# Moving VectorE's additions on product banks, and the sample rows' sums, behind the next unit's parts in a hybrid decoder step

## The chip, the cores and the metric

The kernel runs on one core of one Trainium2 chip. The metric is the device time of one execution in microseconds (us). One execution was taken by the hardware profiler as well; its rows give the start and length of every instruction on TensorE (PE; its weight loads are PEld), VectorE (DVE), ScalarE (ACT), GpSimd (POOL) and the DMA queue of SyncE (SP).

## The reference

One layer of a decoder trunk is computed for 2048 prompt tokens and for 64 sample tokens (8 sequences of 8). A gated recurrence and a short convolution share one input projection; their outputs go through an output projection and a LayerNorm, and then the MLP follows, in which most of the arithmetic lies:

```python
D_MODEL = 1024; SEQ = 2048; DEC_BATCH = 8; DEC_SEQ = 8; D_FF = 4 * D_MODEL

def _layer(x, s_hgrn, conv_buf, ...):
    proj = jnp.einsum('btd,dp->btp', x, w_in)
    ...                                       # recurrence, short convolution, gates
    mix = jnp.einsum('btm,md->btd', jnp.concatenate([o, yc], axis=-1), w_out)
    x = _layer_norm(ALPHA * x + mix, ln1_g, ln1_b)
    hid = jnp.square(jax.nn.relu(jnp.einsum('btd,df->btf', x, w_ff1)))
    x = _layer_norm(ALPHA * x + jnp.einsum('btf,fd->btd', hid, w_ff2), ln2_g, ln2_b)
    return x, s_new, new_buf
```

All is float32. A float32 operand is split into a high part and the rest, and a product is made of three matmuls (high by high, high by low, low by high).

## The kernel before, in words

**Blocks.** The prompt goes in four blocks of 512 tokens (b = 0 to 3); the 64 sample tokens ride along in block 1. Per block come the input projection with the recurrence (phase m), the output projection with the first LayerNorm, and the MLP (phase f). The kernel is scheduled by hand: instructions stand on each engine in the order in which the Python code issues them, and every engine works through its own list in that order.

**The MLP.** The 4096 hidden columns are eight chunks c of 512. The first two chunks of a block (the first four in block 0) are made plainly by `ff1`. The others, and the whole second matrix, are made by seven block products of a 2 by 2 block scheme, named in `PRODUCTS` in the order T4, B11, B21, T2, T1, T3, B22. The chunks go in two parts of four. In a part, first come the first-matrix products of its chunks, seven *units* per chunk (`ff1_product`), and then the second-matrix products, a unit for every product and chunk (28 units, in the loop over `ff2_units`; 21 in the last part of block 3): first T4 for the four chunks, then B11 for the four, and so on. There are thus seven places where a run of `ff1_product` units ends and a run of second-matrix units begins: block 0 part 1, and both parts of blocks 1, 2 and 3.

**A unit's weights.** A unit uses one weight tile of 128 by 1024. `weights(u)` calls `ahead`, which keeps the splitting of weights four tiles ahead: it first runs all that waits in the list `later` (`flush`), and then ScalarE copies the tile that SyncE's DMA brought (`st`, three buffers) to the high part `wh` (L203), and the subtraction that makes the low part `wl` on VectorE (L210) is put into `later`. So the low part stands on VectorE's list only when the next unit begins. `st` is free for the next DMA when `wl` is made. `wh` and `wl` have four buffers each.

**What a first-matrix product leaves behind.** Its matmuls end in one of the PSUM banks D, A, C, B (eight banks in all, handed out in turn). `out(slot, op)` in `ff1_product` brings the bank into a quarter of the chunk's tile `raw`: for T4, B11, T2 and T1 as a copy by ScalarE (L1145); for B21 (one quarter), T3 (two quarters) and B22 (one quarter) as an addition by VectorE (L1147), issued at once behind the unit's matmuls. `sout` does the same for the 64 sample columns in block 1 (L1157). Behind such an addition the square of the rectified quarter (L1111, L1112, two ScalarE instructions) is put into `later`, after B22 also `chunk_done`, a subtraction between quarters on VectorE (L1044).

**What a second-matrix unit needs.** `prepare` splits a quarter of `raw`, two units before its use, into the high part `h` (ScalarE, L164) and the low part `l` (VectorE, L165, by way of `later`). The third matmul of a unit (L247) is the first that needs `l`. In block 1 the units of B11, B21, T1 and B22 also multiply the sample rows: their two parts stand side by side in the tile `hp`, made one unit ahead (L164, L165), and used at the unit's end (L250, L251). `X` is the next block's input, split in the same way between the weights.

**What a second-matrix product leaves behind.** After the last chunk of a product, additions to the output tiles (`add_to`, L1242 and L1245) go into the list `slow`, of which every following unit moves one entry (two if more than four are left) to `later`. `sample_sums` takes the sample rows' bank: ScalarE copies its upper 64 rows to `tmp` (L256), VectorE adds the lower 64 rows (L1252), both at once behind the matmuls, and the additions to the output rows (L1258, L1261) go into `slow`. There are eight such sums. `sum_rows` (L1234) makes sums of quarters that later products need.

**GpSimd in block 0.** It makes the tables of weight sums in DRAM (T_a, T_b) by DMA. To hold these transfers back, `hold` lets GpSimd read an element of slot 0 of `raw` (`tick`, L354) after each of the first eight `ff1_product` units of block 0, and issues one transfer behind it.

Of the kernel before, what the change touches and what calls it, by code (L numbers as in the profile page):

```python
# [14 lines left out]
ALU = mybir.AluOpType  # L15
# [9 lines left out]
NS = 64  # L25
# [4 lines left out]
ALPHA = float(2.0 ** 0.25)  # L30
# [31 lines left out]
def hybrid_step(ctx, tc, a, o):  # L62
    nc = tc.nc
    v, s, g, te = nc.vector, nc.scalar, nc.gpsimd, nc.tensor
# [26 lines left out]
    def TMP():  # L91

        return S((P, 4, P)) if phase["in"] == "m" else new((P, 4, P), "tmp", 2, F32, phase["of"])
# [14 lines left out]
    def PS(shape=(P, 512)):  # L108
        count[0] += 1
        return psum.tile(list(shape), F32, tag="ps", bufs=8, name=f"ps{count[0]}")  # L110
# [42 lines left out]
    later = []  # L153
# [89 lines left out]
    def mm3_on(out, lh, ll, rh, rl, first, last):  # L243

        te.matmul(out, lh, rh, start=first, stop=False, skip_group_check=True)  # L245
        te.matmul(out, lh, rl, start=False, stop=False, skip_group_check=True)  # L246
        te.matmul(out, ll, rh, start=False, stop=last, skip_group_check=True)  # L247
# [5 lines left out]
    def upper(bank):  # L253

        tmp = TMP().rearrange("p a b -> p (a b)")
        s.activation(tmp[:NS], bank[NS:2 * NS, :], AF.Copy)  # L256
        return tmp[:NS]
# [146 lines left out]
    for b in range(NB):  # L404
# [529 lines left out]
        def before():  # L934
            if lnq:
                for f in lnq[0][0]:
                    f()

        def after():
            if lnq:  # L940
                fs = lnq.pop(0)[1]
                if fs:
                    flush()
                for f in fs:
                    f()
# [83 lines left out]
        def sample_values(c, f):  # L1029
            part = c // NPART  # L1030
            if part not in rs:
                rs[part] = TOK().rearrange("p (f t) -> p f t", t=NS)
            return rs[part][:, f % (NPART * FC):f % (NPART * FC) + 2, :]

        def values(c):
            if c not in raw:

                raw[c] = F((P, 4, 2, 256), "raw", NPART)
            return raw[c]

        def chunk_done(c):

            r = raw[c]
            later.append(lambda: v.tensor_tensor(r[:, 0], r[:, 1], r[:, 0], ALU.subtract))  # L1044
# [65 lines left out]
        def relu2(z):  # L1110
            s.activation(z, z, AF.Relu)  # L1111
            s.activation(z, z, AF.Square)  # L1112
# [3 lines left out]
        def ff1_product(step, c, w):  # L1116

            wh, wl = w
            before()
            r = values(c)  # L1120
            k = to[step]
            if k not in fb:
                if samp and k != "D":
                    fb[k] = [PS()[:, :256 + NS] for _ in range(2)]
                else:
                    ps = PS((P, 2, 256))
                    fb[k] = [ps[:, q, :] for q in range(2)] + [ps]
                first = True
            else:
                first = False  # L1130
            banks_ = fb[k]
            xh_, xl_ = xq[step]
            n = 256 + NS if samp and step in SAMPLE else 256
            for kk in range(4):
                for q in range(2):
                    cs = slice(q * 512 + kk * P, q * 512 + kk * P + P)
                    mm3_on(banks_[q][:, :n], wh[:, cs], wl[:, cs], xh_[:, kk, :n], xl_[:, kk, :n],
                           first and kk == 0 and (q == 0 or len(banks_) == 2), kk == 3)

            def out(slot, op):  # L1140

                pairs_ = [(r[:, slot], banks_[2])] if len(banks_) == 3 else [(r[:, slot, q], banks_[q][:, :256]) for q in range(2)]
                for z, ps in pairs_:
                    if op < 2:
                        s.activation(z, ps, AF.Copy, scale=(1.0, -1.0)[op])  # L1145
                    else:
                        v.tensor_tensor(z, z, ps, (ALU.add, ALU.subtract)[op - 2])  # L1147

            def sout(half, op):
                if samp:  # L1150
                    z = sample_values(c, c * FC + 2 * half)
                    for q in range(2):
                        ps = banks_[q][:, 256:]
                        if op < 2:
                            s.activation(z[:, q, :], ps, AF.Copy, scale=(1.0, -1.0)[op])
                        else:
                            v.tensor_tensor(z[:, q, :], z[:, q, :], ps, ALU.add)  # L1157
                    if op == 2:
                        later.append(lambda: relu2(z))

            if step == "T4":
                out(0, 0)
            elif step == "B11":
                out(1, 0)
                sout(0, 0)
                sout(1, 1)
            elif step == "B21":
                out(1, 2)
                sout(0, 2)
                later.append(lambda: relu2(r[:, 1]))  # L1170
            elif step == "T2":
                out(3, 1)
            elif step == "T1":
                out(2, 1)
            elif step == "T3":
                out(2, 3)
                out(0, 2)
                later.append(lambda: relu2(r.rearrange("p (a b) q t -> p a b q t", b=2)[:, :, 0]))
            else:
                out(3, 3)  # L1180
                sout(1, 2)
                later.append(lambda: relu2(r[:, 3]))
                fb.clear()
                if b < NB - 1 or c < NCH - 1:
                    later.append(lambda: chunk_done(c))
            after()
# [60 lines left out]
        slow = []  # L1247

        def sample_sums(bank, into):

            up = upper(bank)
            v.tensor_tensor(up, up, bank[:NS, :], ALU.add)  # L1252

            def add(dh, sign):
                z = x1[NC][:NS, dh * 512:dh * 512 + 512]
                op = ALU.add if sign > 0 else ALU.subtract
                if (NC, dh) in touched:
                    v.tensor_tensor(z, z, up, op)  # L1258
                else:
                    touched.add((NC, dh))  # L1260
                    v.scalar_tensor_tensor(z, z, ALPHA, up, ALU.mult, op)  # L1261

            for dh, sign in into:
                slow.append(lambda dh=dh, sign=sign: add(dh, sign))

        for part, (ff1_units, ff2_units) in enumerate(pl["parts"]):
# [37 lines left out]
            for n_, (step, c, u) in enumerate(ff2_units):  # L1304
# [34 lines left out]
                if c == clast:  # L1339
                    for t0, dh, sign in INTO[k][step]:  # L1340
                        for p in range(2):
                            slow.append(lambda z=(t0 + p, dh, banks[k][p], sign): add_to(*z))
                    if samp and step in SAMPLE:
                        sample_sums(ys, SAMPLE[step][1])
# [7 lines left out]
        if b == NB - 1:  # L1352
# [21 lines left out]
            for t in range(nt):  # L1374
                for dh in range(2):
                    bank = PS()
# [110 lines left out]
```

## Time and profile before

| | |
|---|---|
| median of 3 runs | 2390.7 us (2389.76 to 2390.98) |
| the profiled execution | 2390.55 us, of which 2388.3 us is the span from the first to the last instruction |
| mean granted TensorE clock | 0.994 |
| busy: PE, PEld, DVE, ACT, POOL | 2340.0, 2043.1, 1785.6, 1233.5, 184.9 us |
| VectorE waiting for a product's last matmul, ahead of L1147 | 104.7 us in 57 waits |
| VectorE waiting for `tmp`, ahead of L1252 | 32.6 us in 8 waits |
| first-matrix units of block 2, part 1 | 1661.25 to 1741.88 us |
| second-matrix units of block 2, part 1 | 1741.88 to 1821.13 us |

In a row of the timeline stand an instruction's start in us from the start of the span, its length, engine, line, operation, the tile written and those read, and in brackets how long the engine had been idle before it and what ended that. The records of neighbouring matmuls overlap: in the second-matrix units one starts every 0.23 us and is shown with 0.39 us. So a stall of TensorE is read from the distance between starts; the idle time that a row shows is about 0.16 us less.

### The profile page before, as it was taken

To read this page: it belongs to the slowest core of one execution; us is meant where nothing else is said; L and a number is where in the kernel's file an instruction comes from. 1 tells how busy PE (TensorE), PEld (TensorE's weight loads), DVE (VectorE), ACT (ScalarE), POOL (GpSimd) and SP (SyncE) were. 2 spreads that over 40 slices of the span, in tenths; PEclk is the share of its full clock that TensorE was granted. 3 is DMA by queue.
4 is the path that set the end of the run, shared out by engine and by line. 5 is a ranking of instruction groups with operands and counts; after the bars stand their busy time and mean duration, and the time that the engine had idled before them with its cause. 6 is when DMAs were issued, how large, how long until landed. Compare 5 with 4: busy or idle time off the path is not lost.

```text
span 2388.3 us, 38146 instructions
## 1 busy us (share of the span) xinstructions
PE 2340.0 (98%) x15036; PEld 2043.1 (86%) x15036; DVE 1785.6 (75%) x2832; ACT 1233.5 (52%) x1922; POOL 184.9 (8%) x234
## 2 busy tenths in 40 slices
PE   8999999999999999999999999999999999999998
PEld 7778978988879889879878788998988788998996
DVE  7856858578785677875688956888588975888678
ACT  5324645565423446646654234665665324665563
POOL 2230021100101110000000000000000001000001
PEclk9999999999999999999999999999999999999999
DMA  8997598867633644545553325456665325456663
GB/s 285 264 282 214 151 266 273 257 200 211 163 107 78 172 149 133 168 150 177 177 177 109 99 71 194 155 187 197 192 210 163 102 79 172 141 176 203 200 191 119
DMA packets 131507, 418.89 MB, mean 175 GB/s; under 512 B 13376, under 2 KB 17856, under 8 KB 131328
## 3 DMA queue, kind: packets, MB, share of 16 engines
q1 hardware_dynamic: 108880, 347.96, 45.7%
q0 software_dynamic: 22016, 67.71, 11.5%
q8 instruction: 118, 1.93, 0.3%
q10 hardware_dynamic: 432, 0.79, 0.1%
q14 instruction: 61, 0.50, 0.1%
HBM read 405.36 MB, written 69.77 MB: 199 GB/s over the span
## 4 chain that ended last, share of the span: by engine, by line
PE 50%; DVE 5%; DMA 1%; issue 1%; ACT 1%; POOL 0%; POOLq 0%; DVEq 0%; ACTq 0%
PE ps L247 9%; PE ps L245 9%; PE ps L246 9%; PE ps L239 6%; PE ps L240 6%; PE ps L241 6%; DVE wl L210 1%; DMA st<-in_w_ff 1%; PE ps L683 1%; PE ps L250 1%; PE ps L251 1%; DVE S L603 0%; DMA st<-T_b 0%; DVE l L165 0%; ACT wh L203 0%
## 5 line engine op out<-in xcount | busy, mean ns | idle before, releaser
L210 DVE TENSOR_TENSOR wl<-st,wh 128x1024 fp32r<-128x1024 f32 x580 | 707.4, 1221 | 173.3 <-ACT wh L203 171.2
L203 ACT ACTIVATE wh<-st 128x1024 fp32r<-128x1024 f32 x581 | 612.9, 1055 | 352.1 <-PE ps L247 125.6
L239 PE MATMUL ps<-X,wh 128*128 128x256 f32 (+2 forms) x1376 | 466.6, 339 | 9.8 <-ACT X L164 8.3
L240 PE MATMUL ps<-X,wh 128*128 128x256 f32 (+2 forms) x1376 | 456.8, 332 | 0.3 <-DVE X L165 0.3
L241 PE MATMUL ps<-X,wl 128*128 128x256 f32 (+2 forms) x1376 | 456.3, 332 | 0.0
L247 PE MATMUL ps<-wh,l 128*128 128x512 f32 x868 | 340.8, 393 | 9.0 <-DVE l L165 8.6
L245 PE MATMUL ps<-wh,h 128*128 128x512 f32 x868 | 338.2, 390 | 0.0
L246 PE MATMUL ps<-wl,h 128*128 128x512 f32 x868 | 338.0, 389 | 0.0
L239 PEld LDWEIGHTS ps<-X,wh 128*128 128x128 f32 x1376 | 263.0, 191 | 35.0 <-ACT X L164 9.3
L241 PEld LDWEIGHTS ps<-X,wl 128*128 128x128 f32 x1376 | 262.8, 191 | 22.0
L240 PEld LDWEIGHTS ps<-X,wh 128*128 128x128 f32 x1376 | 263.2, 191 | 21.3 <-DVE X L165 1.5
L247 PEld LDWEIGHTS ps<-wh,l 128*128 128x128 f32 x868 | 162.9, 188 | 52.4 <-DVE l L165 19.0
L246 PEld LDWEIGHTS ps<-wl,h 128*128 128x128 f32 x868 | 163.0, 188 | 34.0
L245 PEld LDWEIGHTS ps<-wh,h 128*128 128x128 f32 x868 | 163.0, 188 | 33.1 <-ACT h L164 0.4
L165 DVE TENSOR_TENSOR l<-raw,h 128x512 fp32r<-128x512 f32 x217 | 148.2, 683 | 9.8 <-ACT h L164 9.8
L247 PE MATMUL ps<-X,wl 128*128 128x256 f32 (+1 forms) x528 | 152.1, 288 | 0.2 <-DVE wl L210 0.2
L246 PE MATMUL ps<-X,wh 128*128 128x256 f32 (+1 forms) x528 | 151.9, 288 | 0.0
L245 PE MATMUL ps<-X,wh 128*128 128x256 f32 (+1 forms) x528 | 151.9, 288 | 0.0
L271 POOL TENSOR_TENSOR sm<-sm,nhalf 128x1 f32<-128x1 f32 (+1 forms) x34 | 34.7, 1020 | 1475.8 <-DVE sm L270 1429.6
L1147 DVE TENSOR_TENSOR raw<-raw,ps 128x512 f32<-128x512 f32 (+1 forms) x112 | 61.0, 571 | 104.9 <-PE ps L247 104.7
L164 ACT ACTIVATE h<-raw 128x512 fp32r<-128x512 f32 x217 | 133.7, 616 | 2.3 <-PE ps L246 2.2
L239 PE MATMUL ps<-wh,X 128*128 128x512 f32 x256 | 105.8, 413 | 2.8 <-DVE S L603 2.8
(259 smaller groups left out, 4369.2 us busy)
## 6 DMA issues: line engine op xcount, KB each, us to landing
st<-in_w_ff SPq DMA_DIRECT2D x227, 512.0 KB, 3.7
st<-T_b SPq DMA_DIRECT2D x124, 512.0 KB, 3.7
st<-in_w_in SPq DMA_DIRECT2D x110, 512.0 KB, 3.9
st<-T_a SPq DMA_DIRECT2D x88, 512.0 KB, 3.5
st<-in_w_out SPq DMA_DIRECT2D x56, 512.0 KB, 4.5
T_b<-in_w_ff POOLq DMA_DIRECT2D x48, 512.0 KB, 14.7
T_a<-in_w_ff POOLq DMA_DIRECT2D x36, 512.0 KB, 19.1
T_b<-T_b POOLq DMA_DIRECT2D x16, 512.0 KB, 12.9
```

Of the source, the lines that this page charges most:

```text
L164: s.activation(hi, src, AF.Copy)
L165: later.append(lambda: v.tensor_tensor(lo, src, hi.bitcast(F32), ALU.subtract))
L203: s.activation(wh, st, AF.Copy)
L210: v.tensor_tensor(wl, st, wh.bitcast(F32), ALU.subtract)
L239: te.matmul(out, lh, rh, start=first, stop=False)
L240: te.matmul(out, lh, rl, start=False, stop=False)
L241: te.matmul(out, ll, rh, start=False, stop=last)
L245: te.matmul(out, lh, rh, start=first, stop=False, skip_group_check=True)
L246: te.matmul(out, lh, rl, start=False, stop=False, skip_group_check=True)
L247: te.matmul(out, ll, rh, start=False, stop=last, skip_group_check=True)
L271: g.tensor_tensor(st[:n, 15:16], st[:n, 14:15], nhalf[:n, 0:1], ALU.pow)
L1147: v.tensor_tensor(z, z, ps, (ALU.add, ALU.subtract)[op - 2])
```

## The change

Three things that stood at once behind a unit's matmuls are put into lists. The additions of `out` and of `sout` go into `later`, and so run when the next unit begins, behind the `wl` that is in the list already. In `sample_sums` ScalarE's copy of the upper rows goes into `later`, and VectorE's addition of the lower rows becomes an entry of `slow`, behind the `add_to` entries and ahead of the additions to the output rows.

```diff
@@ ff1_product: out, sout
                     if op < 2:
                         s.activation(z, ps, AF.Copy, scale=(1.0, -1.0)[op])
                     else:
-                        v.tensor_tensor(z, z, ps, (ALU.add, ALU.subtract)[op - 2])
+
+                        later.append(lambda z=z, ps=ps: v.tensor_tensor(z, z, ps, (ALU.add, ALU.subtract)[op - 2]))
...
                         else:
-                            v.tensor_tensor(z[:, q, :], z[:, q, :], ps, ALU.add)
+                            later.append(lambda z=z[:, q, :], ps=ps: v.tensor_tensor(z, z, ps, ALU.add))
@@ sample_sums
-            up = upper(bank)
-            v.tensor_tensor(up, up, bank[:NS, :], ALU.add)
+            up = []
+            later.append(lambda: up.append(upper(bank)))
+            slow.append(lambda: v.tensor_tensor(up[0], up[0], bank[:NS, :], ALU.add))
...
                 if (NC, dh) in touched:
-                    v.tensor_tensor(z, z, up, op)
+                    v.tensor_tensor(z, z, up[0], op)
                 else:
                     touched.add((NC, dh))
-                    v.scalar_tensor_tensor(z, z, ALPHA, up, ALU.mult, op)
+                    v.scalar_tensor_tensor(z, z, ALPHA, up[0], ALU.mult, op)
```

The order of TensorE's, ScalarE's, GpSimd's and SyncE's instructions stays as it was; VectorE's changes in two kinds of place, and one of GpSimd's instructions waits for something else. The lines behind L1147 move down by one or two (L1147 becomes L1148, L1157 L1158, L1242 L1243, L1252 L1254).

On VectorE, this is where block 2, part 1 goes from the last first-matrix units (T3, B22) to the second-matrix units; before:

```order
L210 TENSOR_TENSOR wl_17063<-st_17033,wh_17035 128x1024
L1147 TENSOR_TENSOR raw_16899<-raw_16899,ps_16932 128x512 x2
L210 TENSOR_TENSOR wl_17095<-st_17065,wh_17067 128x1024
L1147 TENSOR_TENSOR raw_16899<-raw_16899,ps_17037 128x512
L210 TENSOR_TENSOR wl_17128<-st_17099,wh_17101 128x1024
L1044 TENSOR_TENSOR raw_16899<-raw_16899 128x512
L165 TENSOR_TENSOR X_17137<-st_17133,X_17135 128x2x512
L165 TENSOR_TENSOR l_17141<-raw_16669,h_17140 128x512
```

And the same place now:

```order
L210 TENSOR_TENSOR wl_17063<-st_17033,wh_17035 128x1024
L210 TENSOR_TENSOR wl_17093<-st_17065,wh_17067 128x1024
L1148 TENSOR_TENSOR raw_16899<-raw_16899,ps_16932 128x512 x2
L210 TENSOR_TENSOR wl_17127<-st_17099,wh_17101 128x1024
L1148 TENSOR_TENSOR raw_16899<-raw_16899,ps_17037 128x512
L1044 TENSOR_TENSOR raw_16899<-raw_16899 128x512
L165 TENSOR_TENSOR X_17137<-st_17133,X_17135 128x2x512
L165 TENSOR_TENSOR l_17141<-raw_16669,h_17140 128x512
```

T3's two additions (x2) and B22's one each went from ahead of a `wl` to behind it; the rest, `chunk_done` (L1044) and the first `l` among it, stands as it stood. The other chunks' B21, T3 and B22 changed in the same way.

On VectorE in block 1, part 0, at the end of the second-matrix product B11; before:

```order
L165 TENSOR_TENSOR hp_9918<-tok_8945,hp_9918 128x2x64
L1252 TENSOR_TENSOR tmp_9966<-tmp_9966,ps_9870 64x512
L210 TENSOR_TENSOR wl_9969<-st_9941,wh_9943 128x1024
L1234 SCALAR_TENSOR_TENSOR raw_9489<-raw_9489 128x512
L165 TENSOR_TENSOR l_9946<-raw_8754,h_9945 128x512
L165 TENSOR_TENSOR hp_9948<-tok_8945,hp_9948 128x2x64
L210 TENSOR_TENSOR wl_10002<-st_9974,wh_9976 128x1024
L1245 SCALAR_TENSOR_TENSOR tok_8321<-tok_8321,ps_9856 128x512
```

And now:

```order
L165 TENSOR_TENSOR hp_9918<-tok_8945,hp_9918 128x2x64
L210 TENSOR_TENSOR wl_9966<-st_9941,wh_9943 128x1024
L1235 SCALAR_TENSOR_TENSOR raw_9489<-raw_9489 128x512
L165 TENSOR_TENSOR l_9946<-raw_8754,h_9945 128x512
L165 TENSOR_TENSOR hp_9948<-tok_8945,hp_9948 128x2x64
L210 TENSOR_TENSOR wl_10001<-st_9973,wh_9975 128x1024
L1246 SCALAR_TENSOR_TENSOR tok_8321<-tok_8321,ps_9856 128x512
L1246 SCALAR_TENSOR_TENSOR tok_8323<-tok_8323,ps_9857 128x512
L165 TENSOR_TENSOR l_9978<-raw_9227,h_9977 128x512
L165 TENSOR_TENSOR hp_9980<-tok_8945,hp_9980 128x2x64
L210 TENSOR_TENSOR wl_10032<-st_10007,wh_10009 128x1024
L1254 TENSOR_TENSOR tmp_9971<-tmp_9971,ps_9870 64x512
```

The addition of the lower rows left its place ahead of the next unit's `wl`, `l` and `hp` and stands two units later.

On GpSimd in block 0, part 1, with what each instruction waits for; the `tick` behind the unit T3 of the part's first chunk, before:

```order
L354 TENSOR_TENSOR tick<-raw_3934 128x1 [waits Pool_49]
L347 DMA T_b_141<-in_w_ff 128x1024 [waits DMASW2_49]
L354 TENSOR_TENSOR tick<-raw_3934 128x1 [waits DVE_49]
L347 DMA T_b_145<-in_w_ff 128x1024 [waits DMASW3_49]
L354 TENSOR_TENSOR tick<-raw_3934 128x1 [waits Activation_49,Pool_49]
```

And now:

```order
L354 TENSOR_TENSOR tick<-raw_3934 128x1 [waits Pool_49]
L347 DMA T_b_141<-in_w_ff 128x1024 [waits DMASW2_49]
L354 TENSOR_TENSOR tick<-raw_3934 128x1 [waits Pool_49]
L347 DMA T_b_145<-in_w_ff 128x1024 [waits DMASW3_49]
L354 TENSOR_TENSOR tick<-raw_3934 128x1 [waits DVE_49,Activation_49]
```

The second `tick` no longer waits for T3's addition to slot 0, since that addition is issued behind it now; the addition waits for the `tick` instead.

## The prediction

> **What bounds the kernel now.** I read the page first, then TensorE's waits, and then the timeline at the places that the change touches.
>
> ```profile
> span 2388.3 us, 38146 instructions
> PE 2340.0 (98%) x15036; PEld 2043.1 (86%) x15036; DVE 1785.6 (75%) x2832; ACT 1233.5 (52%) x1922; POOL 184.9 (8%) x234
> L1147 DVE TENSOR_TENSOR raw<-raw,ps 128x512 f32<-128x512 f32 (+1 forms) x112 | 61.0, 571 | 104.9 <-PE ps L247 104.7
> ```
>
> TensorE is busy through 98% of the span; 48 us are all that it stands idle. VectorE is busy through 75%, and its 104.7 us of waiting ahead of L1147 cost nothing by themselves: they are worth something only where TensorE waits later for what stood behind them. So TensorE's own waits come next.
>
> ```profile
> PE ps L247 <- DVE l L165: 8.6, 12, 1.4
> PE ps L245 <- ACT raw L1145: 4.5, 2, 3.5
> PE ps L250 <- DVE hp L165: 3.2, 3, 1.3
> ```
>
> These are the waits in the MLP (the rest is in the recurrence and the norm, which the change leaves alone). None is in a run of first-matrix units but the 4.5 us, and those are in block 0:
>
> ```profile
> 1661.20:1741.90 80.70, 80.70 (x674) 80.66 (x674) 46.97 (x50) 51.80 (x67) 0.00 (x0) 1.00 0.59 190
> ```
>
> The columns are the stretch, its length, and the busy time of PE, PEld, DVE, ACT and POOL. The first-matrix units of block 2, part 1 keep TensorE busy for 80.70 of 80.70 us, though 57 waits of VectorE lie in such stretches: there the removed waits were hidden. So the change can win only where `l` and `hp` come late behind a moved instruction, and it can lose wherever a moved instruction now comes late itself.
>
> **The sums of the sample rows (gain).** The second-matrix units of block 1 lie from 978 to 1073 and from 1164 to 1260 us. At the end of B11 in part 0:
>
> ```profile
> 1004.93 0.68 DVE L1252 TENSOR_TENSOR tmp<-tmp,ps 64x512 f32<-64x512 f32 x1 [4.38 <-ACT tmp L256]
> 1005.54 1.21 DVE L210 TENSOR_TENSOR wl<-st,wh 128x1024 fp32r<-128x1024 f32 x1
> 1007.88 0.28 DVE L165 TENSOR_TENSOR hp<-tok,hp 128x128 fp32r<-128x128 f32 x1
> 1008.30 0.47 PE L250 MATMUL ps<-wh,hp 128*128 128x512 f32 x1 [1.31 <-DVE hp L165]
> ```
>
> VectorE stands 4.38 us at L1252; behind it are `wl`, a sum, `l` and `hp`, for whose sources ScalarE had long been done, and TensorE then waits 1.31 us for `hp`. With L1252 moved away these four take some 2.6 us (1005.54 to 1008.16) out of the 4.38 us, and TensorE finds `hp` made. The moved addition costs the same 0.6 us two units later.
>
> ```profile
> PE ps L247 <- DVE l L165: 2.3, 4, 0.6
> ...
> 1182.32 0.49 PE L250 MATMUL ps<-wh,hp 128*128 128x512 f32 x1 [0.56 <-DVE hp L165]
> ```
>
> From 978 to 1260 us TensorE waits 2.3 us in four for `l`, and all the 3.2 us for `hp` of the list above lie there too: 5.5 us in seven waits. The one at 1182.32, 0.56 us, stands behind a split of `X` and stays; the others follow a sum. That is 4.9 us of idle time. The records overlap by 0.16 us, so each stall is that much longer than its row says, and the matmul behind it starts some 0.1 us late; with the short delays that no row of waits names, I put 0.3 us on each of eight places where a sum is made, 2.4 us: **7.3 us** gained. The ends are 5 us and 8.5 us.
>
> **B22's addition where the second-matrix units begin (loss).** This is the place in block 2, part 1:
>
> ```profile
> 1739.28 1.28 DVE L1147 TENSOR_TENSOR raw<-raw,ps 128x512 f32<-128x512 f32 x2 [3.03 <-PE ps L247]
> 1742.09 0.69 DVE L1147 TENSOR_TENSOR raw<-raw,ps 128x512 f32<-128x512 f32 x1 [0.39 <-PE ps L247]
> 1743.73 1.23 DVE L210 TENSOR_TENSOR wl<-st,wh 128x1024 fp32r<-128x1024 f32 x1 [0.95 <-ACT wh L203]
> 1744.87 0.69 DVE L1044 TENSOR_TENSOR raw<-raw 128x512 f32<-128x512 f32 x1
> 1745.87 1.23 DVE L165 TENSOR_TENSOR X<-st,X 128x1024 fp32r<-128x1024 f32 x1 [0.31 <-ACT X L164]
> 1747.01 0.69 DVE L165 TENSOR_TENSOR l<-raw,h 128x512 fp32r<-128x512 f32 x1
> ...
> 1736.82 1.05 ACT L203 ACTIVATE wh<-st 128x1024 fp32r<-128x1024 f32 x1
> 1740.59 1.06 ACT L1111 ACTIVATE raw<-raw 128x1024 f32<-128x1024 f32 x1 [2.73 <-DVE raw L1147]
> 1742.65 1.04 ACT L203 ACTIVATE wh<-st 128x1024 fp32r<-128x1024 f32 x1
> 1743.60 0.62 ACT L1111 ACTIVATE raw<-raw 128x512 f32<-128x512 f32 x1
> 1745.73 0.61 ACT L164 ACTIVATE h<-raw 128x512 fp32r<-128x512 f32 x1
> ...
> 1747.81 0.44 PE L247 MATMUL ps<-wh,l 128*128 128x512 f32 x1
> ```
>
> T3's two additions lose nothing: the `wl` now ahead of them has its `wh` at 1737.87 (1736.82 and 1.05), while VectorE stands idle for 3.03 us, and is done by 1739.1, before TensorE is. So ScalarE's square of T3 (1740.59) and the `wh` behind it (1742.65) stay where they are. B22 is otherwise. The `wl` put ahead of its addition needs that very `wh` and so can't start before 1743.73; 1.14 us later (as 1743.73 to 1744.87) the addition runs, at 1744.87 instead of 1742.09. Its 0.69 us end at 1745.56, and ScalarE's square of B22, which ran at 1743.60 straight behind `wh`, starts at 1745.59: **2.0 us later**. What is queued behind it moves with it: on ScalarE the split of `X`, `h`, the next `wh`; on VectorE `chunk_done` (it needs the square), `X`, `l`. So `l` ends at 1749.7 instead of 1747.70. TensorE's L247 of the third unit took it at 1747.81, without a wait to speak of: slack 0.1 us. So 1.9 us are lost, and not given back, since the later splits moved along.
>
> The same order stands at all seven places; the first and the last of them:
>
> ```profile
> 506.91 1.23 DVE L210 TENSOR_TENSOR wl<-st,wh 128x1024 fp32r<-128x1024 f32 x1 [0.95 <-ACT wh L203]
> 510.19 0.68 DVE L165 TENSOR_TENSOR l<-raw,h 128x512 fp32r<-128x512 f32 x1
> ...
> 2301.14 1.23 DVE L210 TENSOR_TENSOR wl<-st,wh 128x1024 fp32r<-128x1024 f32 x1 [0.96 <-ACT wh L203]
> 2304.42 0.68 DVE L165 TENSOR_TENSOR l<-raw,h 128x512 fp32r<-128x512 f32 x1
> ```
>
> From `wl` to `l` there are 3.28 us in the three, so the slack is alike: 7 x 1.9 = **13.3 us** lost. The ends: 10 us (half a microsecond of slack more in each), and 15 us (in block 1 four small additions stand where one was, 2.1 us each).
>
> **The other additions (at nothing).** Inside a run of first-matrix units B22's addition comes 2 us late too, but what stands behind it is a weight tile for a unit three further on, and ScalarE's copies of the next chunk's banks. The tightest is T2's, whose bank T3 adds to one unit later:
>
> ```profile
> 1575.89 0.58 ACT L1145 ACTIVATE raw<-ps 128x512 f32<-128x512 f32 x1
> ...
> 1578.31 0.28 PE L245 MATMUL ps<-sn,wh 128*128 128x256 f32 x1
> ```
>
> It ends at 1576.47, 1.84 us ahead of T3, and by then ScalarE's idle time has made up a part of the 2.0 us. If it hasn't, 0.2 us are lost at each of the 15 borders between chunks, 3 us in all. B21's additions are like T3's. `wl` being made earlier lets SyncE issue the next `st` some 2 us sooner; with no wait of TensorE for weights there, it is worth nothing.
>
> **Block 0, part 1 (unclear).** Its first two chunks run while transfers are late:
>
> ```profile
> 440.13 1.06 ACT L203 ACTIVATE wh<-st 128x1024 fp32r<-128x1024 f32 x1 [6.06 <-DMA st<-in_w_ff]
> 441.10 1.05 ACT L1111 ACTIVATE raw<-raw 128x1024 f32<-128x1024 f32 x1
> 444.09 0.62 ACT L1111 ACTIVATE raw<-raw 128x512 f32<-128x512 f32 x1
> 457.30 1.06 ACT L203 ACTIVATE wh<-st 128x1024 fp32r<-128x1024 f32 x1 [3.98 <-DMA st<-in_w_ff]
> 429.33 0.81 POOL L347 DMA_DIRECT2D T_b<-in_w_ff  x1 [1.12 <-DMA T_b<-T_b]
> 437.79 0.19 POOL L354 TENSOR_TENSOR tick<-raw 128x1 f32<-128x1 f32 x1 [7.65 <-DVE raw L1147]
> ```
>
> Here `wh` is late itself (440.13), so T3's additions too now wait for a `wl`: its square goes from 441.10 to about 443.7, B22's from 444.09 to about 448.6, and TensorE's next T2 by up to 4 us. Against it, the wait at 457.30 is for a transfer and may swallow that, and the transfers may come sooner by 2 us. GpSimd's `tick` no longer waits 7.65 us for T3's addition; its transfer leaves at about 430 and not at 438, into the same queue. I take **2.5 us** lost, near the middle of -2 us (part of the 4.5 us goes) and +6 us (the 4 us stay, and the third chunk starts late as well).
>
> **The sum.** 2390.55 (2388.3 and 2.25 around it) - 7.3 + 13.3 + 2.5 = **2399.0 us**; the profiled execution is within 0.2 us of the median, 2390.7.
>
> **The rivals.** *Faster:* the seven places cost nothing. The mechanism is that the `wl` ahead of B22's addition is done before TensorE is, as at T3. It decides from the point where its `wh` starts 2 us sooner, at 1740.6 instead of 1742.65; for it speaks that transfers leave earlier, against it that this `wh` stands behind T3's square, which ends at 1742.74 whatever the transfers do. Then 2390.55 - 7.3, and block 0 at nothing: 2383 us. Chance 0.13. *No change:* the losses are half (some 0.9 us of slack that `l` has and I don't see, in each), and block 0 is even: 2390.55 - 7.3 + 6.7 = 2390 us. Chance 0.14. *Slower still:* the new stalls bring the clock down.
>
> ```profile
> 900.00:904.00 4.00, 2.08 (x14) 1.65 (x14) 3.79 (x9) 2.38 (x7) 0.00 (x0) 1.00 0.51 183
> 904.00:908.00 4.00, 4.00 (x19) 4.00 (x19) 3.37 (x3) 0.05 (x1) 0.00 (x0) 0.57 0.00 0
> 456.00:460.00 4.00, 1.10 (x9) 1.10 (x10) 1.23 (x1) 2.31 (x3) 0.00 (x0) 1.00 0.73 282
> ```
>
> The column behind POOL is the granted clock. After a stretch in which TensorE was busy for 2.08 of 4 us it fell to 0.57 for 4 us, which costs 1.7 us; after one with 1.10 of 4 us it stayed at 1.00. So a stall doesn't settle it; five such falls would make 2399.0 + 8.5 = 2407 us. Chance 0.08, with the case that the copies inside the chunks lose their cover. The Trainium skill ("TensorE: Matmul & The Clock Gate", What's actually happening) lets the clock fall after an idle window of some 3.4 us, in windows that run freely; by that rule no stall of 1.9 us would do it. The row at 904 speaks against so simple a rule, the one at 456 not for it.
>
> **How the numbers follow.** My forecast, with its terms between their ends (2393 to 2405), has 0.65. About 0.2%, 4.8 us, is what a measurement of this kernel can tell from no change. The range of 2388 to 2407 us takes in the forecast and the no-change case, and leaves out the faster one and some of the slower. Faster than 2385.8: 0.13. Within: the no-change case and 0.06 of the forecast's low end, 0.20. Slower than 2395.5: 0.67.
>
> **What would show it.** Right: TensorE's waits for `hp` from 978 to 1260 us gone; at the seven places L1044 and the square of B22 2 us later against the `wh` ahead of them, and a wait of TensorE for `l` in the third second-matrix unit, of about 0.9 us for `h` and 0.9 us for `l`; the first-matrix runs outside block 0 still without a wait. Wrong: a `wl` that ends before TensorE does at B22, or first-matrix units that wait.

## The result, and the profile after

| | before | after |
|---|---|---|
| median of the timed runs | 2390.23 us (2389.07 to 2390.98, 4 runs) | 2410.1 us (2407.42 to 2414.41, 4 runs) |
| the profiled execution; its span | 2390.55; 2388.3 us | 2409.96; 2407.7 us |
| mean granted TensorE clock | 0.994 | 0.990 |

The ratio is 1.0087 (95%: 1.0071 to 1.0103): about 20 us slower, where 2399.0 was forecast with 2407 as the upper end. The direction was right and the size was not.

The groups by line show at once that the edit did what it says. First two of before's groups, with the idle time ahead of the group as the last column:

```profile
L210 DVE TENSOR_TENSOR wl<-st,wh 128x1024 fp32r<-128x1024 f32 x580 | 707.4, 1221 | 173.3 <-ACT wh L203 171.2 <-issue 0.3
L1111 ACT ACTIVATE raw<-raw 128x512 f32<-128x512 f32 (+1 forms) x66 | 50.7, 768 | 80.9 <-DVE raw L1147 80.9
```

And after:

```profile
L210 DVE TENSOR_TENSOR wl<-st,wh 128x1024 fp32r<-128x1024 f32 x580 | 708.1, 1221 | 324.5 <-ACT wh L203 322.3 <-issue 0.3 <-PE ps L246 0.2
L1148 DVE TENSOR_TENSOR raw<-raw,ps 128x512 f32<-128x512 f32 (+1 forms) x112 | 60.0, 567 | 0.8
L1111 ACT ACTIVATE raw<-raw 128x512 f32<-128x512 f32 (+1 forms) x66 | 50.9, 772 | 118.3 <-DVE raw L1148 118.3
```

The 104.7 us in which VectorE waited for TensorE ahead of the additions are 0.8 us now. They did not turn into free time: the waiting moved ahead of `wl` (173.3 to 324.5 us; VectorE now waits there for ScalarE), and ScalarE's wait for the additions, ahead of the squares, grew from 80.9 to 118.3 us. What counts is TensorE. Its waits in the MLP after, which answer to the three rows of before (us in total, times, longest):

```profile
PE ps L245 <- ACT h L164: 9.4, 7, 2.8
PE ps L247 <- DVE l L165: 8.1, 12, 1.3
PE ps L245 <- ACT raw L1145: 6.5, 6, 1.9
PE ps L250 <- DVE hp L165: 0.6, 1, 0.6
```

The first row is new: seven waits for `h`, one at each of the seven places where second-matrix units begin. The place of block 2, part 1, again:

```profile
1744.39 1.06 ACT L203 ACTIVATE wh<-st 128x1024 fp32r<-128x1024 f32 x1
1747.94 1.06 ACT L1111 ACTIVATE raw<-raw 128x1024 f32<-128x1024 f32 x1 [2.49 <-DVE raw L1148]
1749.99 1.04 ACT L203 ACTIVATE wh<-st 128x1024 fp32r<-128x1024 f32 x1
1752.93 0.63 ACT L1111 ACTIVATE raw<-raw 128x512 f32<-128x512 f32 x1 [1.89 <-DVE raw L1148]
1755.08 0.61 ACT L164 ACTIVATE h<-raw 128x512 fp32r<-128x512 f32 x1
...
1745.48 1.23 DVE L210 TENSOR_TENSOR wl<-st,wh 128x1024 fp32r<-128x1024 f32 x1 [0.27 <-ACT wh L203]
1746.63 1.28 DVE L1148 TENSOR_TENSOR raw<-raw,ps 128x512 f32<-128x512 f32 x2
1751.07 1.22 DVE L210 TENSOR_TENSOR wl<-st,wh 128x1024 fp32r<-128x1024 f32 x1 [3.17 <-ACT wh L203]
1752.21 0.68 DVE L1148 TENSOR_TENSOR raw<-raw,ps 128x512 f32<-128x512 f32 x1
1752.81 0.68 DVE L1044 TENSOR_TENSOR raw<-raw 128x512 f32<-128x512 f32 x1
1755.20 1.23 DVE L165 TENSOR_TENSOR X<-st,X 128x1024 fp32r<-128x1024 f32 x1 [1.71 <-ACT X L164]
1756.34 0.69 DVE L165 TENSOR_TENSOR l<-raw,h 128x512 fp32r<-128x512 f32 x1
...
1746.05 0.28 PE L245 MATMUL ps<-sw,wh 128*128 128x256 f32 x1
...
1748.93 0.40 PE L245 MATMUL ps<-wh,h 128*128 128x512 f32 x1
...
1755.74 0.50 PE L245 MATMUL ps<-wh,h 128*128 128x512 f32 x1 [1.19 <-ACT h L164]
1757.09 0.80 PE L247 MATMUL ps<-wh,l 128*128 128x512 f32 x1 [0.61 <-DVE l L165]
1757.68 0.63 PE L245 MATMUL ps<-wh,h 128*128 128x512 f32 x1
```

The addition (1752.21) stands behind a `wl` that had to wait 3.17 us for its `wh`. From that `wh` to B22's square there are 2.94 us now (1749.99 to 1752.93); there were 0.95. In TensorE's rows, B22's unit starts at 1746.05 and the second-matrix units at 1748.93; in the third of them it waits 1.19 us for `h` and 0.61 for `l`. The last two starts lie 0.59 us apart where 0.23 is usual: the clock is down.

Where the time went, stage by stage, taken between the starts of the first matmuls of each stage. "Half clock" is the time that stretches of half clock cost in the stage:

| stage | before | after | half clock, after |
|---|---|---|---|
| second-matrix units, block 0 part 1 | 79.38 | 81.85 | 1.71 |
| the same, block 1 parts 0 and 1 | 95.02, 95.67 | 96.88, 94.00 | 3.41, 0 |
| block 2 parts 0 and 1 | 77.18, 79.25 | 80.11, 81.98 | 1.71, 1.71 |
| block 3 parts 0 and 1 | 76.25, 57.24 | 78.54, 61.21 | 0, 1.71 |
| first-matrix units, block 0 part 1 | 86.19 | 89.58 | 1.71 |
| the same, blocks 2 and 3, four stages in all | 241.90 | 246.39 | 0 |
| all else of the span | 1500.3 | 1497.2 | |

The seven second-matrix stages grew by 14.6 us, the four first-matrix stages by 4.5, block 0's by 3.4; the rest, which the change leaves alone almost everywhere, came out 3.1 us shorter in this execution (1.9 of them by less half clock). Each column is one execution.

### The profile page after: what moved, and what is told of

Same layout as the page of the kernel before. It is cut to its first block, busy times and chain, and to the rows that moved or that the text cites. A ratio compares the mean times of both kernels' runs of the same rounds, so it can differ in the third digit from the quotient of the medians.

```text
span 2407.7 us, 38120 instructions
## 1 busy us (share of the span) xinstructions
PE 2352.0 (98%) x15036; PEld 2051.7 (85%) x15036; DVE 1785.5 (74%) x2832; ACT 1230.7 (51%) x1922; POOL 186.3 (8%) x234
## 4 chain that ended last, share of the span: by engine, by line
PE 67%; DMA 11%; DVE 10%; ACT 8%; issue 4%; POOL 0%; POOLq 0%; SPq 0%; ACTq 0%; DVEq 0%
PE ps L239 12%; PE ps L240 12%; PE ps L241 12%; PE ps L247 8%; PE ps L245 8%; PE ps L246 8%; DMA T_a<-in_w_ff 4%; ACT wh L203 4%; DMA st<-in_w_ff 3%; DVE wl L210 3%; DVE raw L1148 2%; ACT raw L1111 2%; DMA T_a<-T_a 1%; DMA st<-T_b 1%; PE ps L250 1%
## 5 line engine op out<-in xcount | busy, mean ns | idle before, releaser
L210 DVE TENSOR_TENSOR wl<-st,wh 128x1024 fp32r<-128x1024 f32 x580 | 708.1, 1221 | 324.5 <-ACT wh L203 322.3
L247 PE MATMUL ps<-wh,l 128*128 128x512 f32 x868 | 343.9, 396 | 8.4 <-DVE l L165 8.1
L247 PEld LDWEIGHTS ps<-wh,l 128*128 128x128 f32 x868 | 165.0, 190 | 51.3 <-DVE l L165 17.2
L247 PE MATMUL ps<-X,wl 128*128 128x256 f32 (+1 forms) x528 | 152.1, 288 | 1.5 <-DVE wl L210 1.5
L1111 ACT ACTIVATE raw<-raw 128x512 f32<-128x512 f32 (+1 forms) x66 | 50.9, 772 | 118.3 <-DVE raw L1148 118.3
```

The costliest lines, as they stand in the source:

```text
L210: v.tensor_tensor(wl, st, wh.bitcast(F32), ALU.subtract)
```

## The experiments

The theory: the loss is B22's addition at the seven places, in two parts, the stall itself and the clock that falls behind it. Its rivals: the additions of T3 and B21 lose it (their `wl` is late, too); the earlier `tick` loses it in block 0, by a transfer that leaves earlier; or the sums' part does not gain what was put down for it.

### The sums alone, and the additions alone

The sums alone, against after: both additions at once again.

```diff
-                        later.append(lambda z=z, ps=ps: v.tensor_tensor(z, z, ps, (ALU.add, ALU.subtract)[op - 2]))
+                        v.tensor_tensor(z, z, ps, (ALU.add, ALU.subtract)[op - 2])
...
-                            later.append(lambda z=z[:, q, :], ps=ps: v.tensor_tensor(z, z, ps, ALU.add))
+                            v.tensor_tensor(z[:, q, :], z[:, q, :], ps, ALU.add)
```

> Kernel: the sample rows' sums moved as in the change, the additions of the first-matrix products left at once behind their matmuls as before. Theory M (the loss is made by B22's addition standing behind the low part at the seven places where second-matrix units begin, and the sums win): 2390.2 - 7.3 = 2383 us, TensorE's waits for hp in block 1 go from 3.2 us to under 1 us. Rival R (the deferred sums are a part of the loss, since their bank and the copy are freed later): 2390 us or more, with waits of TensorE in block 1 that were not there before.

The additions alone, against after: `sample_sums` as in before.

```diff
-            up = []
-            later.append(lambda: up.append(upper(bank)))
-            slow.append(lambda: v.tensor_tensor(up[0], up[0], bank[:NS, :], ALU.add))
+            up = upper(bank)
+            v.tensor_tensor(up, up, bank[:NS, :], ALU.add)
...
```

> Kernel: only the additions of the first-matrix products moved, the sums as before. Theory M: the whole loss without the gain, 2410.1 + 7 = 2417 us, a wait of TensorE of 1.8 to 2.2 us at the third second-matrix unit at all seven places, and about half-speed stretches of 3.4 us behind most of them. Rival R (sums share the loss): 2410 us or less.

Measured: the sums alone 2380.54 us beside 2388.12 of before, ratio 0.9963 (0.9950 to 0.9976): 7.6 us gained. The additions alone 2414.15 us, ratio 1.0097 (1.0082 to 1.0113): 26.0 us lost, where the whole change lost 19.9 (22.4 in a second measurement, further down): the sums give 4 to 6 us there too. So the whole loss is in the additions, and the sums win by themselves: the kernel with the sums alone beats before and after. TensorE's waits in block 1's second-matrix stages, first of after and then of the sums alone:

```profile
PE ps L245 <- ACT h L164: 3.7, 2, 2.8
PE ps L247 <- DVE l L165: 0.6, 1, 0.6
PE ps L250 <- DVE hp L165: 0.6, 1, 0.6
```

```profile
PE ps L250 <- DVE hp L165: 0.6, 1, 0.6
```

Only the wait of 0.6 us for `hp` stays, the one behind the split of `X`; seven waits became one. The two stages went from 95.02 and 95.67 to 91.05 and 91.86 us, 7.8 us in all.

### B22's addition at once again, everywhere or at the seven places

Everywhere, against after; T3's and B21's additions and the sums stay where the change put them (the addition of the sample columns has the same edit):

```diff
-                        later.append(lambda z=z, ps=ps: v.tensor_tensor(z, z, ps, (ALU.add, ALU.subtract)[op - 2]))
+                        def add(z=z, ps=ps):
+                            v.tensor_tensor(z, z, ps, (ALU.add, ALU.subtract)[op - 2])
+
+                        add() if step == "B22" else later.append(add)
```

> Kernel: the changed kernel, but B22's addition at once behind its matmuls as before; B21's and T3's stay deferred. Theory M: the seven stalls (about 2.0 us each, 14 us) go and with them five or six half-speed stretches (1.7 us each, 9 to 10 us): 2410.1 - 24 = 2386 us, perhaps 2383. Rival R2 (any deferred addition costs, T3's and B21's too, since each square and with it each later weight tile comes later): only a third to a half of the loss goes, 2398 to 2403 us.

At the end of a part alone, so that B22's additions inside the runs of first-matrix units stay deferred:

```diff
+                        add() if step == "B22" and c % NPART == NPART - 1 else later.append(add)
```

> Kernel: the changed kernel, but B22's addition at once only for the last chunk of a part, that is at the seven places; inside the runs all additions stay deferred. Theory M: the seven stalls and their half-speed stretches go, the waits for ScalarE's copies inside the runs (some 5 us from 2281 to 2303 us and in block 0) stay: 2386 to 2391 us. Rival R2 (the additions inside the runs carry the loss): 2400 us or more.

Measured, beside 2388.12: everywhere 2384.78 us, ratio 0.9978 (0.9967 to 0.9988); at the end of a part alone 2389.11 us, ratio 1.0001 (0.9991 to 1.0012). Each set against its own runs of before, the change stands at +19.9 us (+22.4 when it was measured again), with B22 at once at the seven places at +1.0, with all of B22 at once at -3.3, and with T3 and B21 at once as well (the sums alone) at -7.6. By these medians the seven places carry 18.9 us (21.4 by the second measurement), B22 inside the runs 4.3, and T3 and B21 4.2; the last is not certain, since the intervals of the last two kernels overlap. TensorE's waits with B22 at once everywhere:

```profile
PE ps L247 <- DVE l L165: 7.1, 9, 1.4
PE ps L245 <- ACT raw L1145: 3.8, 1, 3.8
```

There is no row for `h` any more, and the one wait for L1145 is in block 0. With B22 at once at the end of a part alone, there are more waits for the copies of the banks (three of these seven, 3.9 us, are in block 0):

```profile
PE ps L245 <- ACT raw L1145: 5.3, 7, 1.9
```

The four first-matrix stages of blocks 2 and 3 take 41.05, 81.04, 41.06 and 81.12 us in this kernel, and with B22 at once everywhere 40.32, 80.63, 40.32 and 80.63, as in before: 2.4 us that come from B22's deferred addition inside the runs. The runs cost something behind them, too: the seven second-matrix stages take 554.9 us with B22 at once at the end of a part alone, and 551.1 with B22 at once everywhere, 3.9 us less.

The rival of T3 and B21 is refuted as the main cause of the loss. What shows of it in the profiles lies in block 0, part 1: its first-matrix stage takes 85.2 to 86.4 us in the three profiles of kernels with these additions at once (before, the sums alone, the `tick` alone below), and 89.2 to 95.5 us in the seven with them deferred. B22 doesn't decide there: with B22 at once everywhere the stage takes 91.44 us, at the end of a part alone 90.16.

### The `tick` alone

Before, with the additions put at the head of `later`: VectorE's order stays (only the additions of one unit come in reverse order among themselves), but GpSimd's `tick` no longer waits for T3's addition.

```diff
-                        v.tensor_tensor(z, z, ps, (ALU.add, ALU.subtract)[op - 2])
+                        later.insert(0, lambda z=z, ps=ps: v.tensor_tensor(z, z, ps, (ALU.add, ALU.subtract)[op - 2]))
```

> Kernel: the kernel before, with the additions put at the front of the list instead of issued at once: VectorE's order is as before, and only GpSimd's tick in block 0, part 1 no longer waits for T3's addition, so that its transfer to T_b leaves some 7 us sooner. Theory M (the tick matters little): 2388 us, within 3 us of before, and the change only from 419 to 505 us. Rival T (the earlier transfer delays the weights of the first chunks and makes the waits of the changed kernel there): 2 to 5 us slower, with two waits of TensorE of about 2 us for ScalarE's copies from 419 to 505 us.

Measured: 2388.66 us beside 2388.15, ratio 1.0001 (0.9988 to 1.0013). GpSimd in this kernel:

```profile
430.17 0.48 POOL L354 TENSOR_TENSOR tick<-raw 128x1 f32<-128x1 f32 x1
433.16 0.81 POOL L347 DMA_DIRECT2D T_b<-in_w_ff  x1 [2.50 <-DMA T_b<-T_b]
```

The `tick` runs at 430 and no longer at 437.79, and its transfer leaves at 433. Within the 3 us that the interval leaves open it is worth nothing, and this rival falls.

### The stall filled with work

After, with eight matmuls more in the third second-matrix unit at each of the seven places, ahead of the matmul that waits; they go to a spare bank, and nobody reads it. The stall stays and TensorE works in it, so what comes back is the clock's part.

```diff
+                if n_ == 2 and (b or part):
+                    spare = PS()
+                    for _ in range(8):
+                        te.matmul(spare, ones, parts[0][0], start=True, stop=True, skip_group_check=True)
```

> Kernel: the changed kernel with eight matmuls more into a spare bank (128 by 512, about 1.8 us in all, their result is not used) ahead of the third second-matrix unit at each of the seven places, so that TensorE works through most of the stall. The stall stays as long as it is. Theory C (half of the loss there is the clock: a stretch of the gate's grid in which TensorE is idle for half the time is followed by 3.4 us at half speed): no half-speed stretch begins at the seven places, against six stretches in the profile of the changed kernel, 6 x 1.7 = 10 us less: about 2400 us. Rival (the half-speed stretches don't come of these stalls, or the extra matmuls add to the stall): 2410 us, up to 2423 us.

Measured: 2405.76 us beside 2388.15, ratio 1.0077 (1.0056 to 1.0097). That is a miss for the expected 2400 us, and the interval overlaps that of after itself. So both were measured again, beside each other:

> Kernel: the changed kernel once more, beside the filler on the same chip. Both theories: 2405 to 2410 us where before is 2388, mean granted clock 0.990 to 0.992 where before has 0.995.

> Kernel: the changed kernel with the eight matmuls more ahead of the third second-matrix unit, once more, beside the changed kernel itself. Theory C (the clock has about half of the loss): mean granted clock back at 0.994 to 0.996, and 4 to 10 us less than the changed kernel in the same call; less than the 10 us of the clock where waits for l behind the stall come back that the slow stretches had hidden. Rival: the same time within 2 us.

After came to 2411.02 us beside 2388.59 (2407.70 to 2415.95 in four runs), ratio 1.0092 (1.0076 to 1.0109); the filled kernel to 2405.39 us (2401.66 to 2407.11 in five), ratio 1.0064 (1.0050 to 1.0079). All five runs of the filled one lie below all four of after, though the two intervals still overlap by a little: 5.6 us by the medians. The granted clocks of the runs were 0.989 to 0.993 for after, 0.994 to 0.996 for the filled one and 0.995 on the mean for before. TensorE at the place of block 2, part 1, in the first filled profile, and two stretches of 3.41 us there, cut where half clock can begin (see "The clock" below; stretch, length, busy PE, PEld, DVE, ACT, POOL, then the granted clock):

```profile
1747.74 2.02 PE L1331 MATMUL ps<-wh,ones 128*128 128x512 f32 x8
1749.60 0.39 PE L245 MATMUL ps<-wh,h 128*128 128x512 f32 x1
1749.83 0.39 PE L246 MATMUL ps<-wl,h 128*128 128x512 f32 x1
1750.37 0.50 PE L247 MATMUL ps<-wh,l 128*128 128x512 f32 x1 [0.15 <-DVE l L165]
```

```profile
1746.54:1749.96 3.42, 3.42 (x16) 2.66 (x15) 1.71 (x3) 3.39 (x6) 0.00 (x0) 1.00 0.50 153
1749.96:1753.37 3.41, 3.25 (x15) 2.51 (x14) 3.41 (x5) 2.00 (x4) 0.00 (x0) 1.00 0.65 166
```

TensorE is busy through the stall, no half clock follows, and the time comes only partly back. In this profile the seven second-matrix stages cost 17.5 us more than in the one with B22 at once everywhere (81.23, 94.75, 93.85, 78.51, 82.24, 78.51, 59.47 against 78.89, 91.53, 91.60, 76.23, 79.45, 76.25, 57.15), and none of either has half clock. That is the stall without the clock; after's seven cost 23.5 us more. So the clock's part there is 6.0 us. The second profiles of both kernels (572.5 us in after's seven stages, 568.1 in the filled ones) give 4.3 us, with three stretches of half clock in after's stages where the first had six.

The 17.5 us are not all B22 at the seven places. Against the kernel with B22 at once at the end of a part alone (80.09, 92.42, 91.85, 76.51, 80.09, 76.52, 57.45) the filled stages are 13.6 us longer: 2.0 to 2.3 us at each place and 1.1 in block 0. The other 3.9 us are the ones named above, which B22's deferred additions inside the runs cost in these stages. Each stage is one execution, and the border between the two figures is uncertain by some 1 us: in block 0, part 1, the second-matrix stage took 78.56 to 79.85 us in the four kernels that leave B22 at once everywhere.

## Why the prediction was wrong in size

Two steps failed: that the clock would stay ("So a stall doesn't settle it"), and "The other additions (at nothing)". The stall itself came as it was worked out. The terms, as put and as measured, in the stages of single profiles where nothing else is said:

| term | put | measured |
|---|---|---|
| sums of the sample rows | -7.3 (-5 to -8.5) | -7.8 in the stages, -7.6 timed |
| B22 at the seven places, the stall | 13.3 (10 to 15) | 13.6 |
| the clock behind it | 0 in the forecast | 6.0 (4.3 by the second profiles), 5.6 timed |
| the other additions, in first-matrix stages of blocks 2 and 3 | 0 (up to 3) | 4.5 (2.4 in the second profile of after) |
| the other additions, in the seven second-matrix stages | 0 | 3.9 |
| block 0, part 1, first-matrix units | 2.5 (-2 to 6) | 3.4 (9.3 in the second profile of after) |

Less the 3.1 us of the other stages and 1.1 us by which before's seven stages were longer for other reasons (they took 8.9 us more than with B22 at once everywhere, 7.8 of them for the sums), these make 19.4 us, by which the spans differ. The second profile of after is as long and divides it otherwise: 12.5 us in the seven second-matrix stages, 2.4 in the first-matrix stages of blocks 2 and 3, 9.3 in block 0's, and 4.6 less in the rest.

**The sums** went as worked out, waits and size.

**The seven places.** The mechanism was right. Against the `wh` ahead of it `l` ends 2.0 us later (5.05 us behind its start in before, 7.04 after). From the stage's first matmul to L247 there were 5.93 us in before (1741.88 to 1747.81) and are 8.16 us (1748.93 to 1757.09), 2.2 us more and not 1.9. The other 0.3 us come by way of T3. The `wh` of 1744.39 is 0.5 us later against the stage's start than its fellow of before (1736.82), so the `wl` of 1745.48 is still running when TensorE is done with T3 (1746.05), and the additions start straight behind it (1746.63), where they had waited for TensorE. T3's square and the next `wh` move by 0.3 us with them. "T3's two additions lose nothing" was right even so for T3 by itself: the second-matrix stage of block 2, part 0, takes 76.23 us with T3 deferred and B22 at once everywhere, and 76.25 with the sums alone. T3's additions at that place, with B22 at once everywhere and then with B22 at once at the end of a part alone (T3 is deferred in both):

```profile
1575.69 1.28 DVE L1148 TENSOR_TENSOR raw<-raw,ps 128x512 f32<-128x512 f32 x2
```

```profile
1574.46 1.28 DVE L1148 TENSOR_TENSOR raw<-raw,ps 128x512 f32<-128x512 f32 x2
```

The stage's first matmul is at 1578.37 in the first and at 1576.81 in the second, so that T3's additions start 2.68 us and 2.35 us ahead of it; in before it was 2.61. With B22 at once everywhere they stand at 2.68 us at all five places of blocks 0, 2 and 3; at the end of a part alone at 2.35 to 2.37 at four of the five and at 2.61 in block 2, part 1. So it is B22's deferred addition in the chunks before that makes `wh`, and with it T3, late, and the stage is longer by as much: by 0.28 us in block 2, part 0 (76.51 against 76.23), by 0.27 in block 3, part 0 (76.52 against 76.25). In block 1, where four small additions stand, the filled kernel's part 0 lost 3.2 us (94.75 against 91.53) and part 1 lost 2.3. This, too, comes from the run ahead: with B22 at once at the end of a part, 0.9 and 0.3 us are still lost, and T3's additions start 1.82 us ahead of the stage in part 0 (2.70 with B22 at once everywhere) and 3.68 in part 1 (3.68). The place itself costs 2.3 and 2.0 there. The faster rival is out with this: the `wl` ahead of B22's addition waited 3.17 us for its `wh` and ended long after TensorE did. One detail was wrong and cost nothing: `chunk_done` (L1044) does not wait for B22's square; it ran at 1752.81, ahead of the square. `X` behind it waits for ScalarE, and ScalarE for the square.

**The clock: "So a stall doesn't settle it."** This was the first step that failed. The fall stood as a rival at 8.5 us with a chance of 0.08, on two rows of before that seemed to contradict each other: one with 2.08 of 4 us busy was followed by half clock, one with 1.10 was not. Both stretches were cut at round numbers. Cut at the places where half clock begins, after's rows order themselves:

```profile
446.26:449.67 3.41, 1.51 (x12) 1.31 (x12) 2.58 (x3) 3.25 (x5) 2.00 (x3) 1.00 0.27 70
449.67:453.09 3.42, 3.42 (x19) 3.42 (x18) 1.70 (x2) 1.65 (x3) 0.00 (x0) 0.50 1.01 314
...
1593.14:1596.55 3.41, 1.66 (x7) 0.91 (x6) 2.57 (x3) 3.41 (x5) 0.00 (x0) 1.00 0.30 119
1596.55:1599.97 3.42, 3.42 (x10) 2.65 (x9) 2.73 (x4) 0.86 (x3) 0.00 (x0) 0.50 0.72 237
1753.57:1756.98 3.41, 1.72 (x7) 0.78 (x5) 1.78 (x3) 3.39 (x5) 0.00 (x0) 1.00 0.36 139
1756.98:1760.40 3.42, 3.31 (x8) 2.65 (x9) 3.42 (x5) 1.97 (x4) 0.00 (x0) 0.50 0.69 182
2156.34:2159.75 3.41, 2.28 (x11) 1.55 (x9) 1.70 (x3) 2.83 (x5) 0.00 (x0) 1.00 0.41 154
2159.75:2163.17 3.42, 2.81 (x11) 2.01 (x12) 3.42 (x5) 2.84 (x4) 0.00 (x0) 1.00 0.43 149
2163.17:2166.60 3.43, 3.43 (x17) 2.83 (x16) 2.39 (x3) 1.63 (x3) 0.00 (x0) 1.00 0.79 246
```

The starts of half clock, 449.67, 1596.55 and 1756.98, lie 336 and 47 steps of 3.413 us apart: there is a grid. Where the 2 us stall falls into one of its windows (1.66 and 1.72 us busy), the next window is granted half clock: of its 3.41 us TensorE loses up to 1.7. In block 3, part 0, the same stall is split between two windows (2.28 and 2.81 us busy), and the clock stays. By the rule of the Trainium skill ("TensorE: Matmul & The Clock Gate", What's actually happening), an idle window of some 3.4 us, no stall here could do that; the window's length agrees with the trace (3.41 us), the need for it to be idle does not, since windows that were busy for half their length were followed by half clock.

The price was too simple as well. Five falls at 1.7 us were 8.5 us; the seven stages of after had six, 10.2 us, and only 6.0 of them show; in the second profile three, 5.1 us, and 4.3 of them show. A slow TensorE comes later to waits that it would have met. Block 2, part 1's second-matrix stage shows it; TensorE's waits there in after, which has a fall, and then in the second profile of after, which has none:

```profile
PE ps L247 <- DVE l L165: 1.4, 3, 0.6
PE ps L245 <- ACT h L164: 1.2, 1, 1.2
```

```profile
PE ps L247 <- DVE l L165: 2.4, 3, 0.9
PE ps L245 <- ACT h L164: 1.1, 1, 1.1
```

The slow stretch hides one microsecond of waiting for `l`, and the stage takes 81.98 us with the fall and 82.07 without; what makes up for the rest stays open.

**"The other additions (at nothing)"** failed too. B22's addition inside a run of first-matrix units holds ScalarE's queue for 2 us, and the copies of the next chunk's banks behind it did come late; the sign that the prediction named for it, first-matrix units that wait, is there. In block 3, part 1:

```profile
2302.14 0.59 ACT L1145 ACTIVATE raw<-ps 128x512 f32<-128x512 f32 x1
2302.78 0.39 PE L245 MATMUL ps<-tok,wh 128*128 128x256 f32 x1 [1.34 <-ACT raw L1145]
```

TensorE waits 1.34 us for that copy. The prediction bounded this by 0.2 us at each of 15 borders, 3 us in all, from one border's row. In the four stages came 4.5 us (2.4 in the second profile of after), and behind the runs, where the prediction saw nothing, the 3.9 us of the seven second-matrix stages: ScalarE reaches the end of a run late, as shown for T3 above. With either figure that is more than 3 us; timed, with B22 at once at the end of a part against everywhere, it is 4.3 us. The runs of block 1 stayed as forecast (45.44 and 90.88 us, unchanged to the hundredth).

**Block 0, part 1.** Its 3.4 us lie within the ends, which was in part luck: the stage took 95.51 us in the second profile of after, 9.3 more than before and beyond the upper end. 1.7 us of the 3.4, and 3.4 of the 9.3, are half clock. That T3's late additions lose time here, as the prediction had it, fits the ten profiles (three with T3 and B21 at once at 85.2 to 86.4 us, seven with them deferred at 89.2 to 95.5); B22's share can't be told from this scatter. That the earlier `tick` does it is excluded by its own run.

## What to carry to other kernels

An instruction that waits at the head of a queue is no loss until somebody misses what stands behind it: 104.7 us of waiting went away here, and what had been released early, B22's addition, was put behind an instruction that waits for a third engine. Before deferring an operation, ask what stands ahead of it in the new place and who is released by it, and move only those operations that release nobody soon (the sums here: 0.9963 by themselves). An operation that is late by little in every round can also leave an engine late where the next phase begins: 3.9 us here. And price a new stall of TensorE together with the clock: with about half of a 3.41 us window idle, the next one could come at half clock, for up to 1.7 us more.

## What the runs showed of the hardware

Half clock came by windows of a fixed grid of 3.413 us, and a partly idle window sufficed. In the ten profiles of this study, from the first matmul to 10 us before the end, of the windows at full clock of which TensorE's records fill at most the share 0.47, all 41 were followed by a window of half clock; with a share of 0.48 to 0.57, 14 of 31 were; with 0.58 to 0.85, none of 161. In the last 10 us of a kernel, 10 of 11 windows with at most 0.47 were. The records of matmuls overlap, so the middle band may be the blur of the measure. Since the grid does not follow the program, the same stall is followed by half clock in one execution and not in the next: at the place of block 2, part 1, the clock fell in the first profile of after (1.72 us busy) and did not in the second, whose window and the next were:

```profile
1757.75:1761.16 3.41, 1.96 (x8) 0.98 (x6) 1.70 (x3) 3.38 (x6) 0.00 (x0) 1.00 0.41 144
1761.16:1764.58 3.42, 3.12 (x14) 2.59 (x15) 3.42 (x5) 2.00 (x4) 0.00 (x0) 1.00 0.59 170
```
